# Turning u token-major with VectorE's 32 by 32 block transpose and a placing store, instead of TensorE's transpose through PSUM

## The chip, the cores and the metric

The kernel runs on one core of one Trainium2 chip. The metric is the device time of one execution in microseconds (us). Three executions of the kernel before took 592.72, 593.20 and 593.23 us: median 593.2.

## The reference

One decoder layer over 1024 tokens of width 1024, in float32. The normalised stream goes through one input projection into two head groups, a state-space layer (S5) and a latent attention (MLA); their outputs, 512 wide each, are concatenated, and then:

```python
mix = jnp.concatenate([ys, ym], axis=-1) @ w_out[i]
u = DEEPNORM_ALPHA * x + mix
ple = jax.nn.sigmoid(u @ w_pg[i]) * (p[i] @ w_pp[i])
x = layer_norm(u + ple, ln_g[i], ln_b[i])
```

So `u` is used twice: as an operand of the gate's matmul `u @ w_pg`, and as an addend beside the gate's result.

## The kernel before, in words

**Layout.** Up to the output projection everything is feature-major: 128 features on the partitions, tokens along the free axis. The gate's matmul makes token-major results (128 tokens on the partitions, 512 columns), and so does everything behind it. `u` is needed in both layouts: feature-major as the stationary operand of the gate's matmul, token-major as the addend. This case is about how the token-major copy is made.

**Precision.** Each float32 operand of a matmul is split into a high and a low part (`split`, line 511: a cast makes the high part, a subtraction the low one), and each product is three matmuls (`mm3`, line 518): high by high, high by low, low by high.

**Output projection (`out_proj`, line 1310).** There are eight blocks `m` of 128 features and two halves `hf` of 512 tokens. For each, 8 x 3 = 24 matmuls of 128x512 add up in one PSUM bank (`op`). VectorE then makes u in place in `xr` (`stt`, line 1319: alpha times the stream plus the bank), and `split` makes `uh` and `ul`, the operands of the gate. The weights `wor` and the stream `xr` are loaded two blocks ahead (`wo_load`), and the weights are split one block ahead (`wo_split`, to `woh` and `wol`).

**Token-major u (`u_tokens`, line 1322).** After both halves of a block, for each half: four TensorE transposes of 128x128 by an identity matrix into one PSUM bank (`ut`), one ScalarE copy from PSUM to the tile `ut` (128 tokens by 4 times 128 features), and one store of 256 KB to the DRAM tensor `d_ut`, whose rows are tokens. One row of this store is 128 features, 512 bytes.

**Gate (`gate`, line 1360).** For each of eight token blocks `t` and two column halves `c`, 8 x 3 = 24 matmuls (`g`), with the weights `wph` and `wpl` (loaded as `wpr`, four pieces for each column half, each of which serves two of the eight steps). ScalarE takes the sigmoid into `sgg`, VectorE multiplies it by the stored per-layer embedding (`ppr`) and adds the token-major u, which `u_load` (line 1352) loads back from `d_ut` as `utok` in 2 KB rows. `final` normalises the rows and stores the output. The first three token blocks run their column half 0 before their column half 1 (`GATE`, line 97).

**What sets the order.** The kernel doesn't issue its instructions directly. `Plan` (line 120) records all of them, with costs for each operation (`cost`), and `issue` (line 308) simulates the engines and writes down one order: at each step the earliest instruction that can start, with the written order as priority. Each engine then runs its own instructions strictly in that order. All DMAs go out on SyncE's queue (SP), also in order. Every DMA signals on one of eight completion semaphores in turn, and a DMA waits for the one issued eight before it.

**Buffers.** Tiles of 128x512 come from a pool of 12 (`Hf`), tiles of 128x1024 from a pool of 40 (`U`), the banks for `op` and `ut` from a pool of four (`PB`).

All instructions have line 441 in the profile, because the plan issues them there. So groups are told apart by the names of their tiles.

Of the kernel before, what the change touches and what calls it, by code (L numbers as in the profile page):

```python
# [34 lines left out]
P = 128  # L35
# [409 lines left out]
def trunk(ctx, tc, I, out):  # L445
    plan = Plan(tc)
    V, A, Gp, T, SY = plan.vector, plan.scalar, plan.gpsimd, plan.tensor, plan.sync
# [12 lines left out]
    def nm(s):  # L460
        cnt[0] += 1
        return f"{s}{cnt[0]}"
# [4 lines left out]
    def Hf(name, dt=F32, shape=(P, 512)):  # L467
        return plan.own(hp.tile(list(shape), dt, name=nm(name), tag="h"), "h", NHF)

    def C(name, shape, dt=F32):  # L470
        return cp.tile(list(shape), dt, name=nm(name), tag=nm(name))
# [7 lines left out]
    def PB(name, shape=(P, 512), dt=F32):  # L479
        return plan.own(psB.tile(list(shape), dt, name=nm(name), tag="B"), "B", 4)  # L480
# [27 lines left out]
    def cpy(e, o, a):  # L508
        plan.copy(e._name, o, a)
# [35 lines left out]
    def pexp(o, x, shape):  # L545
# [22 lines left out]
    ident = C("ident", (P, P))  # L568
    Gp.memset(ident, 1.0)
    Gp.affine_select(  # L570
        out=ident, in_=ident, pattern=[[-1, P]], compare_op=ALU.is_equal, fill=0.0, base=0, channel_multiplier=1
# [20 lines left out]
    d_ut = dr.tile([8, P, D], F32, name="d_ut")  # L592
# [702 lines left out]
    wo = {}  # L1295
# [24 lines left out]
        split(uT[m][0][:, s], uT[m][1][:, s], x[:, s])  # L1320

    def u_tokens(m, hf):
        x = wo[m][2]
        ps = PB("ut")
        for j in range(4):
            T.transpose(ps[:, j * P : j * P + P], x[:, hf * 512 + j * P : hf * 512 + j * P + P], ident)
        t = Hf("ut", shape=(P, 4, P))
        cpy(A, t, ps.rearrange("p (j c) -> p j c", j=4))
        SY.dma_start(out=d_ut[hf * 4 : hf * 4 + 4, :, m * P : m * P + P].rearrange("t p c -> p t c"), in_=t)


    wp = {}
# [189 lines left out]
    for i in range(n + 3):  # L1522
        if i < n:
            h, j = items[i]
            pr[i] = [scores(h, 2 * j + q) for q in range(2)]
        k = i - 1
        if 0 <= k < n:
            pts[k] = probs_t(*items[k], pr.pop(k))
        k = i - 2
        if 0 <= k < n:  # L1530
            os[k] = pv(*items[k], pts.pop(k))
        k = i - 3
# [3 lines left out]
    for m in range(NK):  # L1536
        if m + 2 < NK:
            wo_load(m + 2)
        if m + 1 < NK:
            wo_split(m + 1)  # L1540
        for hf in range(2):
            out_proj(m, hf)
        for hf in range(2):
            u_tokens(m, hf)
        if m == 6:
            for k in range(4):
                wp_load(0, k)
# [79 lines left out]
```

## Time and profile before

| what | value |
|---|---|
| the runs shown | 592.72 to 593.23 us, median 593.2 |
| the profiled execution itself | 592.97 us |
| its span, first to last instruction | 591.3 us |
| mean granted TensorE clock | 0.992 |
| busy: TensorE, VectorE, ScalarE, GpSimd | 567.1, 446.8, 281.6, 83.8 us |
| DMA traffic | 76.66 MB in 46233 packets |
| transposes `ut` on TensorE | 64, first at 411.9 us, last at 496.0 us |
| copies `ut` on ScalarE | 16, 588 ns each |
| stores `d_ut` | 16 of 256 KB, 2.4 us from issue to landing |

How to read it: the profiled execution takes 1.7 us more than its span, for what lies before its first and after its last instruction. Times in the views are counted from the span's start. A row of a timeline gives start, duration, engine and the operation as out<-in; in brackets, how long the engine had idled and for whom. PE is TensorE, PEld its weight loads, DVE VectorE, ACT ScalarE, POOL GpSimd, SP the queue of DMAs. Matmuls overlap, so the step from one to the next is less than the duration of one.

### The profile page before, as it was taken

To read this page: it belongs to the slowest core of one execution; us is meant where nothing else is said; L and a number is where in the kernel's file an instruction comes from. 1 tells how busy PE (TensorE), PEld (TensorE's weight loads), DVE (VectorE), ACT (ScalarE), POOL (GpSimd) and SP (SyncE) were. 2 spreads that over 40 slices of the span, in tenths; PEclk is the share of its full clock that TensorE was granted. 3 is DMA by queue.
4 is the path that set the end of the run, shared out by engine and by line. 5 is a ranking of instruction groups with operands and counts; after the bars stand their busy time and mean duration, and the time that the engine had idled before them with its cause. 6 is when DMAs were issued, how large, how long until landed. Compare 5 with 4: busy or idle time off the path is not lost.

```text
span 591.3 us, 8335 instructions
## 1 busy us (share of the span) xinstructions
PE 567.1 (96%) x3000; PEld 482.3 (82%) x3000; DVE 446.8 (76%) x952; ACT 281.6 (48%) x533; POOL 83.8 (14%) x100
## 2 busy tenths in 40 slices
PE   8989989999999999999999999899999999999994
PEld 6777868788898878878899998688888888888884
DVE  6999999989999986478989879876323226577666
ACT  5777136355383851367677786443222235133221
POOL 0000004201020234114522221010000010000000
PEclk9999989999999999999999999899999999999998
DMA  8897422532130512201013225326422438724301
GB/s 301 316 354 267 159 72 86 201 124 95 72 111 2 172 64 72 72 38 37 1 50 129 72 73 171 150 73 247 115 99 72 161 107 278 309 89 160 108 35 72
DMA packets 46233, 76.66 MB, mean 130 GB/s; under 512 B 4384, under 2 KB 27104, under 8 KB 46192
## 3 DMA queue, kind: packets, MB, share of 16 engines
q1 hardware_dynamic: 46192, 76.14, 37.3%
q8 instruction: 23, 0.38, 0.3%
q14 instruction: 18, 0.15, 0.1%
HBM read 50.47 MB, written 25.66 MB: 129 GB/s over the span
## 4 chain that ended last, share of the span: by engine, by line
PE 57%; DVE 4%; issue 1%; ACT 1%; DVEq 0%
PE op L441 15%; PE g L441 15%; PE s L441 6%; PE o L441 4%; PE z L441 4%; PE glu L441 3%; PE pt L441 2%; PE qn L441 2%; PE ut L441 1%; PE uv L441 1%; PE qrp L441 1%; DVE gsr L441 1%; PE y L441 1%; DVE p L441 1%; DVE hh L441 0%
## 5 line engine op out<-in xcount | busy, mean ns | idle before, releaser
L441 PE MATMUL z<-xh,wh 128*128 128x512 f32 x192 | 76.4, 398 | 1.2 <-DVE krh L441 1.2
L441 PE MATMUL z<-xh,wl 128*128 128x512 f32 x192 | 75.7, 396 | 1.1 <-DVE wl L441 1.1
L441 PE MATMUL z<-xl,wh 128*128 128x512 f32 x192 | 76.4, 398 | 0.0
L441 PE MATMUL g<-wph,uh 128*128 128x512 f32 (+1 forms) x136 | 51.4, 378 | 0.0
L441 PE MATMUL g<-wph,ul 128*128 128x512 f32 (+1 forms) x136 | 51.2, 377 | 0.0
L441 PE MATMUL g<-wpl,uh 128*128 128x512 f32 (+1 forms) x136 | 51.2, 377 | 0.0
L441 DVE SCALAR_TENSOR_TENSOR xr<-xr,op 128x512 f32<-128x512 f32 x16 | 11.0, 687 | 50.2 <-PE op L441 50.2
L441 PEld LDWEIGHTS z<-xh,wl 128*128 128x128 f32 x192 | 36.5, 190 | 8.6 <-DVE wl L441 1.7
L441 PEld LDWEIGHTS z<-xh,wh 128*128 128x128 f32 x192 | 36.5, 190 | 8.6 <-DVE krh L441 1.5
L441 PEld LDWEIGHTS z<-xl,wh 128*128 128x128 f32 x192 | 36.6, 190 | 6.9
L441 PEld LDWEIGHTS g<-wph,ul 128*128 128x128 f32 x136 | 25.6, 188 | 4.7
L441 PEld LDWEIGHTS g<-wpl,uh 128*128 128x128 f32 x136 | 25.6, 188 | 4.7
L441 PEld LDWEIGHTS g<-wph,uh 128*128 128x128 f32 x136 | 25.6, 188 | 4.6
L441 DVE CUSTOM_DVE_ANT_0 p<-s,mask 128x128 f32<-128x128 f32 (+7 forms) x32 | 23.8, 752 | 4.0 <-PE s L441 3.8
L441 ACT COPY ut<-ut 128x512 f32<-128x512 f32 x16 | 9.4, 588 | 35.3 <-PE ut L441 35.2
L441 PE MATMUL op<-ysh,woh 128*128 128x512 f32 x64 | 26.2, 409 | 0.0
L441 ACT ACTIVATE p<-p,mx 128x128 f32<-128x128 f32 (+7 forms) x32 | 24.8, 775 | 2.7 <-DVE mx L441 2.6
L441 DVE TENSOR_TENSOR ptl<-pt,pth 128x512 fp32r<-128x512 f32 (+3 forms) x48 | 25.3, 551 | 0.9 <-ACT pth L441 0.4
L441 ACT ACTIVATE sgg<-g 128x512 f32<-128x512 f32 (+1 forms) x17 | 9.6, 565 | 34.0 <-PE g L441 34.0
L441 PE MATMUL pt<-ident,p 128*128 128x128 f32 x144 | 21.5, 285 | 3.8 <-ACT sg L441 2.2
L441 PE MATMUL op<-ysh,wol 128*128 128x512 f32 x64 | 25.0, 391 | 0.0
L441 POOL TENSOR_TENSOR rstd<-ve,half 128x1 f32<-128x1 f32 (+1 forms) x10 | 7.1, 714 | 126.2 <-DVE ve L441 107.6
(370 smaller groups left out, 1673.1 us busy)
## 6 DMA issues: line engine op xcount, KB each, us to landing
wr<-in_w_fm SPq DMA_DIRECT2D x12, 512.0 KB, 5.6
x<-in_x SPq DMA_DIRECT2D x8, 512.0 KB, 8.7
d_pp<-ppo SPq DMA_DIRECT2D x8, 512.0 KB, 4.8
d_xln<-xt SPq DMA_DIRECT2D x16, 256.0 KB, 6.1
wor<-in_w_out SPq DMA_DIRECT2D x8, 512.0 KB, 5.8
xr<-d_xln SPq DMA_DIRECT2D x8, 512.0 KB, 5.2
d_ut<-ut SPq DMA_DIRECT2D x16, 256.0 KB, 2.4
utok<-d_ut SPq DMA_DIRECT2D x16, 256.0 KB, 4.2
```

Source lines behind the costliest of these rows:

```text
L441: getattr(self.real[ran[i]], method)(*ops[i]["args"], **kw)
```

## The change

`u_tokens` no longer uses TensorE, PSUM and ScalarE. VectorE transposes the 128x512 half of `xr` in one instruction, within blocks of 32 by 32: element (32a + k, 32b + i) of the source goes to (32a + i, 32b + k). Partition 32a + i of the tile then holds, for each of the 16 token groups b, the 32 features of feature group a for token 32b + i. Four stores, one for each feature group a, place these runs of 32 features (128 bytes) into the rows of `d_ut`: each store takes 32 partitions and moves 512 runs, 64 KB. `d_ut` holds the same as before, and the loads `utok` are the same. The plan is not edited; it makes its order anew from the changed list of instructions.

```diff
     def u_tokens(m, hf):
-        x = wo[m][2]
-        ps = PB("ut")
-        for j in range(4):
-            T.transpose(ps[:, j * P : j * P + P], x[:, hf * 512 + j * P : hf * 512 + j * P + P], ident)
-        t = Hf("ut", shape=(P, 4, P))
-        cpy(A, t, ps.rearrange("p (j c) -> p j c", j=4))
-        SY.dma_start(out=d_ut[hf * 4 : hf * 4 + 4, :, m * P : m * P + P].rearrange("t p c -> p t c"), in_=t)
+        t = Hf("ut")
+        V.transpose(t, wo[m][2][:, hf * 512 : hf * 512 + 512])
+        for a in range(4):
+            o = d_ut[hf * 4 : hf * 4 + 4, :, m * P + 32 * a : m * P + 32 * a + 32]
+            SY.dma_start(
+                out=o.rearrange("t (b i) k -> i (t b) k", i=32),
+                in_=t[32 * a : 32 * a + 32].rearrange("i (b k) -> i b k", k=32),
+            )
```

In the order of the changed kernel the transposes appear on VectorE as `STREAM_TRANSPOSE ut<-xr`, the stores on SP as four `d_ut<-ut` of 32x16x32.

## The prediction

> **What bounds the kernel now.** First the page: its first part gives the engines' shares, its fourth the chain that ended last.
>
> ```profile
> span 591.3 us, 8335 instructions
> PE 567.1 (96%) x3000; PEld 482.3 (82%) x3000; DVE 446.8 (76%) x952; ACT 281.6 (48%) x533; POOL 83.8 (14%) x100
> PE op L441 15%; PE g L441 15%; PE s L441 6%; PE o L441 4%; PE z L441 4%; PE glu L441 3%; PE pt L441 2%; PE qn L441 2%; PE ut L441 1%; PE uv L441 1%; PE qrp L441 1%; DVE gsr L441 1%; PE y L441 1%; DVE p L441 1%; DVE hh L441 0%
> ```
>
> TensorE sets the time, and the transposes that the change removes (`ut`) stand on the chain themselves, with 1% of it. The change touches one stage, the output projection, so I read that stage alone: the table of stretches (the four busy columns are PE, weight loads, DVE, ACT, then POOL; after them granted clock, DMA share, GB/s), and the chain in order of time.
>
> ```profile
> 401.00:496.00 95.00, 95.00 (x451) 78.74 (x451) 33.69 (x45) 26.32 (x41) 3.50 (x2) 1.00 0.41 138
> 401.10 10.91 PE op L441 x48
> 413.58 10.23 PE op L441 x45
> ...
> 484.46 10.24 PE op L441 x45
> 496.28 86.71 PE g L441 x405
> ```
>
> In these 95 us TensorE is busy throughout at a granted clock of 1.00; VectorE works 33.7 us, ScalarE 26.3, the DMA engines have 41% of their time filled. The chain is `op` with small holes, then 86.7 us of `g` without one. The holes are `ut`. So time taken from TensorE here is time taken from the kernel, as long as nothing else becomes late.
>
> **What is removed from TensorE.** The price is not the duration of a transpose, because matmuls overlap; it is what the next matmul is pushed back. TensorE's timeline:
>
> ```profile
> 400.94 0.40 PE L441 MATMUL op<-ysh,woh 128*128 128x512 f32 x1
> ...
> 411.62 0.40 PE L441 MATMUL op<-ymh,wol 128*128 128x512 f32 x1
> 411.85 0.60 PE L441 MATMUL ut<-ident,xr 128*128 128x128 f32 x4
> 412.20 0.48 PE L441 MATMUL op<-ysh,woh 128*128 128x512 f32 x1
> ...
> 494.54 0.60 PE L441 MATMUL ut<-ident,xr 128*128 128x128 f32 x4
> 494.90 0.48 PE L441 MATMUL g<-wph,uh 128*128 128x512 f32 x1
> ```
>
> From 400.94 to 411.62 lie 47 steps without a transpose: 10.68 / 47 = 0.2272 us a matmul. The first group of `ut` of block 0 starts at 411.85, that of block 7 at 494.54: (494.54 - 411.85) / 7 = 11.81 us a block. A block has 48 matmuls, 10.91 us, so its two groups of transposes cost 0.906 us. Eight blocks: **7.25 us**. (64 transposes at their mean duration would be 17 us; that is no saving, since most of it overlaps.) The order of TensorE where the stage ends and the gate begins (`op` is the last projection group, `g` the first gate group, `ut` the transposes), before:
>
> ```order
> L441 MATMUL op_1186<-ymh_1036,wol_1170 128x512
> L441 MATMUL ut_1187<-ident_75,xr_1158 128x128 x4
> L441 MATMUL g_1203<-wph_1191,uh_1102 128x512
> L441 MATMUL g_1203<-wpl_1192,uh_1102 128x512
> L441 MATMUL g_1203<-wph_1191,ul_1103 128x512
> L441 MATMUL ut_1189<-ident_75,xr_1158 128x128 x4
> L441 MATMUL g_1203<-wph_1191,uh_1114 128x512
> ```
>
> and with the change:
>
> ```order
> L441 MATMUL op_1172<-ymh_1036,wol_1158 128x512
> L441 MATMUL g_1187<-wph_1175,uh_1102 128x512
> L441 MATMUL g_1187<-wpl_1176,uh_1102 128x512
> L441 MATMUL g_1187<-wph_1175,ul_1103 128x512
> L441 MATMUL g_1187<-wph_1175,uh_1112 128x512
> ```
>
> Nothing but `ut` has gone; all other matmuls keep their order. The gate would then start at 400.94 + 384 x 0.2272 = 488.2 instead of 494.9 (the last group of `ut` lies behind three gate matmuls).
>
> ScalarE loses 16 copies out of PSUM. Worth nothing by itself: ScalarE waits for TensorE before them.
>
> ```profile
> L441 ACT COPY ut<-ut 128x512 f32<-128x512 f32 x16 | 9.4, 588 | 35.3 <-PE ut L441 35.2
> ```
>
> **What VectorE gets.** 16 transposes of 128x512 f32. The trace has none; the bounds are a one-input cast, the fastest row of this size, and four times a 128-element scan, the slowest per element:
>
> ```profile
> L441 DVE CAST uh<-xr 128x512 fp32r<-128x512 f32 x1 | 0.4, 426 | 0.0
> L441 DVE SCALAR_TENSOR_TENSOR xr<-xr,op 128x512 f32<-128x512 f32 x15 | 10.3, 687 | 49.2 <-PE op L441 49.2
> L441 DVE TENSOR_TENSOR ul<-xr,uh 128x512 fp32r<-128x512 f32 x15 | 10.4, 692 | 11.0 <-ACT uh L441 11.0
> L441 DVE TENSOR_TENSOR wol<-wor,woh 128x1024 fp32r<-128x1024 f32 x6 | 7.8, 1309 | 0.0
> L441 DVE TENSOR_TENSOR_SCAN rt<-mg,rt 128x128 f32<-128x128 f32 x32 | 12.1, 442 | 0.0
> ```
>
> So 0.43 to 1.77 us; I take 0.69, the f32 rate of most rows. A block asks of VectorE 2 x 0.687 + 2 x 0.692 + 1.309 = 4.1 us, with two transposes 5.4, at most 7.6, of 10.9 us: hidden. In each half the transpose is issued ahead of `ul`, so `ul` and what follows slip by 0.69. In most blocks no one soon needs `ul`. The one tight place is the start of the gate, whose first group needs the low parts `wpl` of the gate weights. VectorE's order there, before:
>
> ```order
> L441 SCALAR_TENSOR_TENSOR xr_1158<-xr_1158,op_1183 128x512
> L441 TENSOR_TENSOR ul_1185<-xr_1158,uh_1184 128x512
> L441 TENSOR_TENSOR wpl_1194<-wpr_1180,wph_1193 128x1024
> L441 TENSOR_TENSOR wpl_1196<-wpr_1181,wph_1195 128x1024
> L441 SCALAR_TENSOR_TENSOR xr_1158<-xr_1158,op_1186 128x512
> L441 TENSOR_TENSOR wpl_1198<-wpr_1182,wph_1197 128x1024
> ```
>
> and with the change:
>
> ```order
> L441 SCALAR_TENSOR_TENSOR xr_1148<-xr_1148,op_1169 128x512
> L441 STREAM_TRANSPOSE ut_1173<-xr_1148 128x512
> L441 TENSOR_TENSOR ul_1171<-xr_1148,uh_1170 128x512
> L441 TENSOR_TENSOR wpl_1178<-wpr_1166,wph_1177 128x1024
> L441 TENSOR_TENSOR wpl_1180<-wpr_1167,wph_1179 128x1024
> L441 SCALAR_TENSOR_TENSOR xr_1148<-xr_1148,op_1172 128x512
> L441 TENSOR_TENSOR wpl_1182<-wpr_1168,wph_1181 128x1024
> L441 TENSOR_TENSOR ul_1171<-xr_1148,uh_1170 128x512
> ```
>
> Block 7's second transpose moved behind all this; its first stands ahead of two `wpl`. In the trace:
>
> ```profile
> 489.30 0.69 DVE L441 SCALAR_TENSOR_TENSOR xr<-xr,op 128x512 f32<-128x512 f32 x1 [4.10 <-PE op L441]
> 490.73 0.69 DVE L441 TENSOR_TENSOR ul<-xr,uh 128x512 fp32r<-128x512 f32 x1 [0.74 <-ACT uh L441]
> 491.34 2.35 DVE L441 TENSOR_TENSOR wpl<-wpr,wph 128x1024 fp32r<-128x1024 f32 x2
> ```
>
> VectorE idles 0.74 us there for ScalarE's `uh`, room for a 0.69 us transpose. The two `wpl` end 4.4 us after `xr` began, and `xr` begins one group, 24 x 0.2272 = 5.45 us, ahead of the gate: they end some 1.0 us before it. Each `wpl` serves six matmuls of a gate group; these two are first read by the 8th and the 14th, 1.6 and 3.0 us into it. So a transpose of 1.77 us, 1.0 more than fits, still costs nothing; TensorE would wait only beyond some 4.5 us. Term: 0.
>
> **What the stores become.** 16 stores of 256 KB in 512-byte rows become 64 of 64 KB in 128-byte runs, four per half block, all on SP's queue. Issue, from two loads issued back to back, is 0.455 us each; 64 of them 29 us of an 80 us stage. SP's order at the stage's end (`wpr` are gate weights, `utok` the loads that read the stored tokens back), before:
>
> ```order
> L441 DMA wpr_1182<-in_w_pg 128x1024
> L441 DMA d_ut<-ut_1176 128x4x128
> L441 DMA d_ut<-ut_1178 128x4x128
> L441 DMA ppr_1199<-d_pp 128x1024
> L441 DMA wpr_1200<-in_w_pg 128x1024
> ```
>
> and with the change:
>
> ```order
> L441 DMA wpr_1168<-in_w_pg 128x1024
> L441 DMA d_ut<-ut_1163 32x16x32 x4
> L441 DMA d_ut<-ut_1164 32x16x32 x4
> L441 DMA d_ut<-ut_1173 32x16x32 x4
> L441 DMA ppr_1183<-d_pp 128x1024
> L441 DMA wpr_1184<-in_w_pg 128x1024
> ```
>
> The weights for the gate's second column half are now queued behind block 7's first stores as well, and the last two of them also behind the `utok` loads that wait until those stores have landed. A store takes 2.4 us from issue to landing now. The price of a 128-byte packet written to DRAM is in no row. The nearest are the 512-byte stores of now (436 to 440 us, two `d_ut`) and a load with 128-byte rows (24 to 25 us, `fr`), and for the rate of large loads the stretch from 497.4:
>
> ```profile
> 450.86 0.91 SPq L441 DMA_DIRECT2D utok<-d_ut  x2
> ...
> d_ut<-ut SPq DMA_DIRECT2D x16, 256.0 KB, 2.4
> ...
> q1 hardware_dynamic: 1056, 0.52, 43.6%
> ...
> fr<-in_inv_freq SPq DMA_DIRECT2D x1, 16.0 KB, 2.5
> q1 hardware_dynamic: 153, 0.02, 11.9%
> ...
> 497.40:503.00 5.60, 5.60 (x27) 4.62 (x26) 3.68 (x4) 3.05 (x4) 0.00 (x0) 1.00 1.04 364
> ```
>
> 0.436 x 4 us x 16 engines / 1056 = 26.4 ns a packet of 512 bytes; 0.119 x 1 us x 16 / 153 = 12.4 ns a packet of 128 (16 KB in 128 rows, the rest signals). Each store has 512 data packets, 32 an engine, and one that signals: 33. At 12.4 ns all 64 take 26 us of each engine, at 26.4 ns 56 us, against 14 us now. I take about 20 ns, between the two rows, 42 us: it fits beside the loads, and no load is late.
>
> The page "DMA: Bandwidth & Descriptors" of the Trainium skill (Specifications) speaks against the change here: under 512 bytes a transfer is not at line rate, because the DMA engine reads, modifies and writes. If that doubled the 26.4 ns of the larger packet, the first rival below would come true; if it doubled 12.4 ns, the sum would stay. No run here shows it yet.
>
> **Sum.** 592.97 us (the profiled execution, of which 591.3 are its span) - 7.25 + 0 + 0 = 585.7. The median of the runs shown is 0.2 us above the profiled one, so I forecast **585.9 us**.
>
> **Rivals.**
>
> *The small stores fill the DMA engines, and the gate waits for weights: slower.* Stores could start at 407.8 (400.94, one group of 5.45, `xr` and a transpose of 0.69 each). Ahead of the last two gate weights stand 60 stores and, with these two, 18 times 512 KB of loads (two `wor`, two `xr`, eight `wpr`, three `ppr`, six `utok` of half the size), at 364 GB/s 1.44 us each, 26 us. With 2 us of latency, and 2.3 for the split of the weights (a cast and a subtraction, rows below), they are ready at 438.1 + 60 x 0.033 x p, p in ns. They are wanted three groups and six steps into the gate, 488.2 + 16.4 + 4.1 = 508.7. Nothing is late below p = 36; the whole gain is gone at 39; at 52.8 (twice the measured 512-byte packet) the wait is 34 us, so 620 us.
>
> ```profile
> L441 ACT CAST wph<-wpr 128x1024 fp32r<-128x1024 f32 x4 | 4.0, 1052 | 0.0
> L441 DVE TENSOR_TENSOR wpl<-wpr,wph 128x1024 fp32r<-128x1024 f32 x2 | 2.4, 1218 | 0.0
> ```
>
> For it: a write is not the load that gave 12.4 ns, and all runs of one store lie at multiples of 4 KB. Against: it takes three times the price of a 128-byte load. Chance 0.12.
>
> *Part of the gain is lost at the gate's start,* to late `wpl` or late gate weights at p between 36 and 39: up to 6 us lost, 587.4 to 592. Against: the margins above. Chance 0.08.
>
> *The change does nothing for the time:* another engine ends the stage where TensorE did. VectorE would need 3.4 us a transpose (10.9 - 4.1, halved); the slowest row says 1.77. 593 us, chance 0.05.
>
> **How the numbers follow.** The forecast, 584.3 to 587.4, has 0.75; its low end lets more close up than the 7.25 us read from the block starts, its high end lets 1.5 us go at the gate. A measurement of this kernel tells 0.2%, 1.2 us, from no change: faster 0.75 + 0.08, same 0.05, slower 0.12. The range 584.3 to 590.0 leaves out the first and third rival and half of the second, near 0.2.
>
> **What would show it.** Right: `ut` gone from TensorE, `op` as one run of 384 matmuls at 0.227 us, `g` from about 488, a transpose near 0.69 us, VectorE still waiting for `op`, packets of 128 bytes at 12 to 27 ns. Wrong: holes in `g` that end with a `wpr` landing or `wph`, a DMA share near 1 from 410 on, `d_ut` landings far above the present 2.4 us, or TensorE waiting for `wpl`.

## The result, and the profile after

The changed kernel takes **585.19 us** (median of four executions, 584.48 to 586.96); the kernel before, run beside it, 592.96. The ratio is 0.987, interval 0.985 to 0.988: some 7.8 us faster. The forecast was 585.9, in a range of 584.3 to 590.0.

The execution profiled took 585.17 us. Its page: the first line, the two lines on TensorE and on DMA traffic that differ most from before, and the shares of the chain.

```profile
span 583.5 us, 8264 instructions
PE 559.1 (96%) x2936; PEld 475.9 (82%) x2936; DVE 457.5 (78%) x968; ACT 272.8 (47%) x517; POOL 83.6 (14%) x100
DMA packets 71577, 76.67 MB, mean 131 GB/s; under 512 B 37920, under 2 KB 52448, under 8 KB 71536
PE g L441 15%; PE op L441 15%; PE s L441 6%; PE z L441 4%; PE o L441 4%; PE glu L441 3%; PE pt L441 2%; PE qn L441 2%; PE uv L441 1%; PE qrp L441 1%; DVE gsr L441 1%; PE y L441 1%; DVE p L441 1%; DVE hh L441 0%; PE qrt L441 0%
```

TensorE has 64 instructions fewer, VectorE 16 more, ScalarE 16 fewer. The same bytes go in 25,000 packets more. `ut` has left the chain. In order of time the chain through both stages is now two rows:

```profile
401.06 87.07 PE op L441 x384
488.13 87.36 PE g L441 x408
```

Before, the same matmuls stood in pieces with the transposes between them, and the last long piece of `g` began at 496.28. The table of stretches (PE, weight loads, DVE, ACT, POOL, clock, DMA share, GB/s) over the projection:

```profile
401.00:488.00 87.00, 87.00 (x386) 72.03 (x385) 41.93 (x57) 18.40 (x26) 3.51 (x2) 1.00 0.55 134
```

TensorE is busy throughout, as it was, in a stretch 8 us shorter. VectorE has 8.2 us more and ScalarE 7.9 less. The DMA engines are at 0.55 instead of 0.41. To find where the time went, I take the first `op` and the fourth gate matmul (in both kernels nothing of `ut` comes after it). TensorE's timeline:

```profile
400.90 0.40 PE L441 MATMUL op<-ysh,woh 128*128 128x512 f32 x1
...
487.96 0.39 PE L441 MATMUL g<-wph,uh 128*128 128x512 f32 x1
488.64 0.39 PE L441 MATMUL g<-wph,uh 128*128 128x512 f32 x1
```

and the same gate matmul before (the first `op` of before, at 400.94, is shown in the prediction):

```profile
496.04 0.47 PE L441 MATMUL g<-wph,uh 128*128 128x512 f32 x1
```

From 400.90 to 488.64 are 87.74 us; before, from 400.94 to 496.04, 95.10. The stretch is 7.36 us shorter, 0.460 for each of the 16 groups. From there to the end of the gate's chain it is 86.85 against 86.95, and the tail behind it 8.01 against 8.31. Together 7.36 + 0.10 + 0.30 + 0.04 (the earlier start) = 7.80, the difference of the two spans.

### The profile page after: what moved, and what is told of

Its sections match the earlier page's. It is cut to its first block, busy times and chain, and to the rows that moved or that the text cites. A ratio compares the mean times of both kernels' runs of the same rounds, so it can differ in the third digit from the quotient of the medians.

```text
span 583.5 us, 8264 instructions
## 1 busy us (share of the span) xinstructions
PE 559.1 (96%) x2936; PEld 475.9 (82%) x2936; DVE 457.5 (78%) x968; ACT 272.8 (47%) x517; POOL 83.6 (14%) x100
## 4 chain that ended last, share of the span: by engine, by line
PE 56%; DVE 5%; issue 1%; ACT 1%; DVEq 0%
PE g L441 15%; PE op L441 15%; PE s L441 6%; PE z L441 4%; PE o L441 4%; PE glu L441 3%; PE pt L441 2%; PE qn L441 2%; PE uv L441 1%; PE qrp L441 1%; DVE gsr L441 1%; PE y L441 1%; DVE p L441 1%; DVE hh L441 0%; PE qrt L441 0%
## 5 line engine op out<-in xcount | busy, mean ns | idle before, releaser
L441 DVE SCALAR_TENSOR_TENSOR xr<-xr,op 128x512 f32<-128x512 f32 x16 | 11.0, 686 | 39.1 <-PE op L441 39.1
L441 ACT CAST uh<-xr 128x512 fp32r<-128x512 f32 x16 | 9.9, 621 | 64.8 <-DVE xr L441 51.5
L441 PE MATMUL op<-ysh,woh 128*128 128x512 f32 x64 | 24.9, 389 | 0.0
L441 PE MATMUL op<-ysl,woh 128*128 128x512 f32 x64 | 24.9, 389 | 0.0
L441 PE MATMUL op<-ymh,woh 128*128 128x512 f32 x64 | 24.9, 389 | 0.0
L441 PE MATMUL op<-yml,woh 128*128 128x512 f32 x64 | 24.9, 389 | 0.0
```

What stands on the lines that cost most here:

```text
L441: getattr(self.real[ran[i]], method)(*ops[i]["args"], **kw)
```

## The experiments

**The theory:** the whole gain is TensorE's time, 0.45 us for each group of four transposes that TensorE no longer does. VectorE's transpose and the 64 small stores lie beside other work and cost nothing. **Rivals:** the gain is larger, and VectorE's transpose or the stores give part of it back; or it comes from ScalarE's copies; or the stage is close to being bound by VectorE, by packets or by the issue of stores.

**How they are compared.** The spans differ by up to 3.8 us before the projection starts, in a part whose instructions stand in the same order in all these kernels: there the granted clock varies, 0.97 to 1.00 between 300 and 400 us. So beside the medians stands the time from the first `op` to the end of the span ("rest"), from the profiled executions, and, as a part of it, the time from the first `op` to the fourth gate matmul ("stage"). The ratios are to the kernel before as it was run beside each kernel (medians 592.41 to 594.01).

| run | first `op` | span | rest | stage | median | ratio to before |
|---|---|---|---|---|---|---|
| before | 400.9 | 591.3 | 190.4 | 95.10 | 592.96 | 1 |
| after | 400.9 | 583.5 | 182.6 | 87.74 | 585.19 | 0.985 to 0.988 |
| e4_te_back | 400.7 | 590.8 | 190.1 | 95.12 | 592.99 | 0.997 to 1.001 |
| e3_half | 402.2 | 588.7 | 186.5 | 91.58 | 590.40 | 0.990 to 0.995 |
| e2_no_turn | 401.3 | 584.2 | 182.9 | 87.75 | 585.81 | 0.983 to 0.988 |
| e1_rows | 404.4 | 587.2 | 182.8 | 87.74 | 587.34 | 0.984 to 0.991 |
| e5_turn_x4 | 401.4 | 584.0 | 182.6 | 87.74 | 585.44 | 0.985 to 0.989 |
| e5_turn_x8 | 400.8 | 585.5 | 184.7 | 87.74 | 587.43 | 0.989 to 0.992 |
| e6_store_x2 | 400.6 | 583.2 | 182.6 | 87.74 | 585.77 | 0.986 to 0.990 |
| e6_store_x4 | 401.9 | 641.0 | 239.1 | 110.30 | 642.49 | 1.081 to 1.085 |
| e7_packets_a | 401.4 | 584.3 | 182.9 | 87.74 | 586.52 | 0.988 to 0.993 |
| e8_packets_b | 402.4 | 627.8 | 225.4 | 100.19 | 629.26 | 1.058 to 1.063 |

All edits are to the changed kernel's `u_tokens`.

### Is it TensorE's time?

**e4_te_back:** the transposes on TensorE come back, into a bank that nobody reads; no copy, and the new transposes and stores stay.

```diff
+        x = wo[m][2]
+        ps = PB("ut")
+        for j in range(4):
+            T.transpose(ps[:, j * P : j * P + P], x[:, hf * 512 + j * P : hf * 512 + j * P + P], ident)
         t = Hf("ut")
         V.transpose(t, wo[m][2][:, hf * 512 : hf * 512 + 512])
```

> The changed kernel, with TensorE's 64 transposes put back beside VectorE's; nobody reads their PSUM banks, and ScalarE's 16 copies and the 512-byte stores stay away. Theory (the gain is TensorE's own time, 16 groups of 0.45 us): 592.4 to 593.2 us, all of the gain gone, no difference to the kernel before. Rival (ScalarE's copies, the PSUM banks held by them, or the new order of the queues bring part of it): clearly under 591 us.

Measured: 592.99 us, ratio 0.997 to 1.001, rest 190.1, stage 95.12 against 95.10 before. The whole gain is gone, though the copies are not back. The chain at the first two blocks and at the gate:

```profile
400.90 10.92 PE op L441 x48
411.82 0.44 PE ut L441 x4
412.25 0.70 PE op L441 x3
412.95 0.44 PE ut L441 x4
...
496.10 86.71 PE g L441 x405
```

Each group of `ut` stands on the chain with 0.44 us, and each leaves the next matmul some 0.02 us later. TensorE waits for nothing else in the stage, so the PSUM banks that `ut` takes up again cost nothing either. So ScalarE's copies were worth nothing, and the new transposes and stores cost nothing.

**e3_half:** the first half of each block in the old way, the second in the new.

```diff
+        if hf == 0:
+            x = wo[m][2]
+            ps = PB("ut")
...
+        else:
+            t = Hf("ut")
+            V.transpose(t, wo[m][2][:, hf * 512 : hf * 512 + 512])
...
```

> Half 0 of every block turned as before (TensorE, PSUM, ScalarE, one store), half 1 as in the changed kernel. Theory: the cost is a fixed one for each group of four transposes, so half of the 7.8 us: 588.9 to 589.5 us. Rival (the gain hangs on one place, such as the start of the gate): near 585 or near 593 us, not between.

Measured: rest 186.5, the middle of 190.4 and 182.6; stage 91.58, 3.84 above the changed kernel's. The median, 590.40, is above what I expected, by about as much as the projection of the profiled execution starts late (1.3 us). The chain:

```profile
402.40 10.91 PE op L441 x48
413.31 0.44 PE ut L441 x4
...
493.28 87.42 PE g L441 x408
```

One group for each block is left, again 0.44 us. The gain is in proportion to the groups removed.

### What do VectorE's transpose and the small stores cost?

**e2_no_turn:** no transpose anywhere; the half of `xr` is stored as it is, in rows of 512 bytes, so `d_ut` no longer holds u by tokens.

```diff
-        t = Hf("ut")
-        V.transpose(t, wo[m][2][:, hf * 512 : hf * 512 + 512])
...
+        x = wo[m][2][:, hf * 512 : hf * 512 + 512]
+        SY.dma_start(out=d_ut[hf * 4 : hf * 4 + 4, :, m * P : m * P + P].rearrange("t p c -> p t c"), in_=x.rearrange("p (j c) -> p j c", j=4))
```

> Leaves the turning out: the feature-major half goes to the scratch tensor as it is, in one store of 512-byte rows, so that neither VectorE nor TensorE nor ScalarE does anything for it. Theory (VectorE's transposes and the small runs are hidden): 584.8 to 585.8 us, the same as the changed kernel. Rival (either of them costs something on the path): faster than the changed kernel, by 1 us or more.

**e1_rows:** the transpose stays, but one store of 256 KB in rows of 512 bytes takes the place of the four; the blocks are not placed.

```diff
-        for a in range(4):
...
+        SY.dma_start(out=d_ut[hf * 4 : hf * 4 + 4, :, m * P : m * P + P].rearrange("t p c -> p t c"), in_=t.rearrange("p (j c) -> p j c", j=4))
```

> VectorE's transposes stay, but each half is stored by one DMA of 256 KB in 512-byte rows, without placing the blocks (the placing is left out). Theory (64 stores of 128-byte runs take some 10 us more of each DMA engine, none of it waited for): 584.8 to 585.8 us, the same as the changed kernel. Rival (the four stores for each half delay something by their issue or their landing): faster than the changed kernel by 1 us or more.

Measured: rest 182.9 and 182.8, against 182.6 with everything; the stage is the same in all three (87.74 to 87.75), and the 0.3 lies behind VectorE's last instruction. The median of e1_rows, 587.34, is above what I expected. Its profiled execution, the slowest of four (588.96), starts the projection at 404.4; of the other three (585.29 to 588.56) no trace was kept. The stretches of e2_no_turn, then those of e1_rows:

```profile
401.00:488.00 87.00, 87.00 (x387) 72.09 (x386) 32.93 (x44) 18.21 (x25) 3.48 (x2) 1.00 0.45 143
```

```profile
404.50:491.50 87.00, 87.00 (x386) 72.01 (x385) 41.99 (x57) 18.44 (x26) 3.50 (x2) 1.00 0.44 140
```

VectorE's column falls by 9 us without the transposes, and the DMA share by 0.1 without the small stores. TensorE's column doesn't move. Neither of the two new costs is on the path.

### How far off are they?

**e5_turn_x4 and e5_turn_x8:** the transpose is done 4 or 8 times (below with 8).

```diff
-        V.transpose(t, wo[m][2][:, hf * 512 : hf * 512 + 512])
+        for _ in range(8):
+            V.transpose(t, wo[m][2][:, hf * 512 : hf * 512 + 512])
```

> Each of VectorE's transposes done four times over (2.85 us a half at 0.712 us each); the result is the same. Theory (VectorE has 5.45 us a half and some 2.0 us of other work; at the start of the gate 3.8 us may slip): nothing is waited for, 584.8 to 586.2 us. Rival (the margin at the gate is less, or the transposes hold up other engines): slower than the changed kernel by 2 us or more, with waits for wpl or ul in g.

> Each of VectorE's transposes done eight times over (5.7 us a half; with xr 6.4 us, against the 5.45 us that TensorE needs for a half). The plan moves ul and wol to GpSimd. Theory: VectorE becomes the bound of the stage, 16 x 0.9 = 15 us more or beyond, 599 to 615 us. Rival (TensorE is buffered well enough by the four PSUM banks for this to stay hidden): under 590 us.

Measured: 4 times cost nothing (rest 182.6), 8 times 2.1 us (184.7). For 8 my theory fell: it took 6.4 us for a half, a sum of durations, and let the excess over 5.45 count in full. The stretch, GpSimd's group in it, and rows of VectorE's timeline:

```profile
401.00:488.00 87.00, 87.00 (x385) 72.01 (x385) 85.55 (x137) 17.50 (x26) 28.09 (x19) 1.00 0.49 128
```

```profile
L441 POOL TENSOR_TENSOR ul<-xr,uh 128x512 fp32r<-128x512 f32 x14 | 18.2, 1298 | 56.7 <-ACT uh L441 46.7 <-issue 9.8 <-PE op L441 0.2
```

```profile
407.33 0.68 DVE L441 SCALAR_TENSOR_TENSOR xr<-xr,op 128x512 f32<-128x512 f32 x1
...
469.18 4.85 DVE L441 STREAM_TRANSPOSE ut<-xr 128x512 f32<-128x512 f32 x8
...
489.97 0.66 DVE L441 SCALAR_TENSOR_TENSOR xr<-xr,op 128x512 f32<-128x512 f32 x1
```

VectorE is full (85.6 of 87 us), and yet TensorE is busy for all 87. Two things let it. The plan has moved the subtractions `ul` to GpSimd. And VectorE's instructions overlap too: eight transposes in a row take 4.84 to 5.46 us here, not eight times a duration. From the first `xr` to the last, VectorE takes (489.97 - 407.33) / 15 = 5.51 us a half, where TensorE gives it 24 x 0.2272 = 5.45. So it hardly falls behind: each `xr` begins 0.5 to 2.4 us after the last matmul of its half, the last one 1.9 us after it. The wait comes only at the gate, for a `wpl` that GpSimd makes behind the last `ul` (TensorE's timeline; in brackets the wait and for whom):

```profile
487.67 0.39 PE L441 MATMUL op<-ymh,wol 128*128 128x512 f32 x1
...
495.06 0.50 PE L441 MATMUL g<-wpl,uh 128*128 128x512 f32 x1 [1.11 <-POOL wpl L441]
```

With that wait the gate takes 1.5 us more than in the changed kernel; the other 0.6 of the 2.1 lies behind VectorE's last instruction, and I know no cause for it.

**e6_store_x2 and e6_store_x4:** each store is made again, once or three times, to DRAM tensors that nobody reads.

```diff
-            SY.dma_start(
-                out=o.rearrange("t (b i) k -> i (t b) k", i=32),
...
+            for d in (o, *(e[hf * 4 : hf * 4 + 4, :, m * P + 32 * a : m * P + 32 * a + 32] for e in d_ux)):
+                SY.dma_start(
+                    out=d.rearrange("t (b i) k -> i (t b) k", i=32),
...
```

> Each of the 64 stores issued twice, the second to a spare tensor that nobody reads: 128 stores. In the changed kernel's trace a 128-byte packet takes 11.6 ns of an engine, so this is as if one took 23 ns, and 128 issues of 0.49 us are 63 us of an 80 us stage. Theory (nothing is late below 36 ns a packet, 0.7 us of issue for each of 64): 584.8 to 586.5 us. Rival (the margin is smaller than was worked out, by the queue's order or the eight stores in flight): slower than the changed kernel by 2 us or more.

> Each of the 64 stores issued four times, three of them to spare tensors: 256 stores, as if a packet took 46 ns, and 256 issues of 0.49 us are 125 us against a stage of 87 us. Theory: the last gate weights are late, by 438 + 60 x 0.033 x 46 - 509 = 20 us if the DMA engines bind, by 408 + 240 x 0.49 + 18 x 0.45 + 7 - 509 = 32 us if the issue on SP binds; 605 to 618 us, with holes in g that end with a wpr. Rival (the loads find their way past the stores, or the plan moves them ahead): under 592 us.

Measured: 128 stores cost nothing (rest 182.6); 256 cost 56 us (239.1). Stretches of e6_store_x2:

```profile
401.00:488.00 87.00, 87.00 (x386) 72.01 (x385) 41.67 (x58) 18.25 (x26) 3.48 (x2) 1.00 0.78 171
```

and of e6_store_x4, with its SP queue (start, duration of the issues) and its chain:

```profile
409.00:505.00 96.00, 80.17 (x354) 66.06 (x352) 33.17 (x48) 11.78 (x18) 0.00 (x0) 0.93 0.72 131
```

```profile
409.71 1.59 SPq L441 DMA_DIRECT2D d_ux<-ut  x3
411.35 0.49 SPq L441 DMA_DIRECT2D d_ut<-ut  x1
411.88 1.58 SPq L441 DMA_DIRECT2D d_ux<-ut  x3
...
505.14 0.46 SPq L441 DMA_DIRECT2D wpr<-in_w_pg  x1
```

```profile
559.43 5.03 DMA wpr<-in_w_pg
```

With twice the stores of e6_store_x2 the DMA share isn't higher, 0.72 against 0.78: the engines aren't the limit. SP is. It issues four stores in 2.17 us (409.71 to 411.88), 0.54 each. The first gate weights go out at 505.1, where they went out at 459.0 in the changed kernel; TensorE's longest wait, 21.6 us up to 510.8, is for them. The last four stand behind 240 stores, 130 us at this pitch, and go out from 559.4 on. The waits of this kernel that show it (us in total, times, longest):

```profile
ACT wph L441 <- DMA wpr<-in_w_pg: 69.5, 8, 24.6
...
PE g L441 <- ACT wph L441: 43.2, 4, 21.6
```

The kind of loss was foreseen, its size was under: 43 of the 56 us are these waits, and 3.2 are one for `sgg`. The others fall together with a granted clock that drops once TensorE idles, 0.93 in the stretch above against 1.00; what it costs I did not separate.

**e7_packets_a and e8_packets_b:** one more store for each half, to a tensor that nobody reads, in pieces of 32 bytes: 4096 pieces in the first (below), 8192 in the second. That adds many packets and only 16 issues.

```diff
+        SY.dma_start(out=d_ux[2 * m + hf][:, :, 0:8], in_=t[:, 0 : 256].rearrange("p (r k) -> p r k", k=8))
```

> The changed kernel with one more store for each half block: 4096 pieces of 32 bytes of the same tile to a spare tensor that nobody reads. Only 16 more issues on SP, but 256 more packets for each DMA engine and half: with the 11.6 ns of the changed kernel's stores 48 us more of each engine, as if every packet of the 64 stores took 34 ns. Theory (the engines have room up to 36 ns): 584.8 to 588 us. Rival (stores four times over were slow because the DMA engines were full, and that happens earlier than worked out): slower than the changed kernel by 5 us or more.

> The same with 8192 pieces of 32 bytes for each half block: 95 us more of each DMA engine, as if a packet took 57 ns, still only 16 more issues. Theory (the DMA engines are the second limit, beyond 36 ns, by the sum of the prediction's first rival): 438 + 60 x 0.033 x 57 - 509 = 42 us late, 615 to 635 us, with holes in g that end with gate weights. Rival (only the issue on SP can be a limit): under 592 us.

Measured: 4096 pieces cost 0.3 us from the projection on (rest 182.9), 8192 cost 43 us (225.4). Stretches of e7_packets_a:

```profile
407.00:488.00 81.00, 81.00 (x359) 67.11 (x358) 36.28 (x51) 15.98 (x22) 2.42 (x1) 1.00 0.90 134
```

and of e8_packets_b, with its waits:

```profile
407.00:488.00 81.00, 81.00 (x359) 67.10 (x358) 34.47 (x49) 12.44 (x18) 0.00 (x0) 1.00 0.94 104
488.00:530.00 42.00, 21.73 (x64) 15.25 (x63) 6.01 (x7) 5.12 (x6) 2.34 (x1) 0.67 0.96 114
```

```profile
PE g L441 <- ACT wph L441: 26.0, 4, 9.5
PE g L441 <- DVE wpl L441: 4.0, 5, 1.6
PE g L441 <- POOL wpl L441: 1.6, 1, 1.6
```

With the DMA engines 90% busy, the stage is as long as in the changed kernel. Once the work in front of the weights no longer ends in time, it still doesn't show in the projection (TensorE is busy 81 of 81 us) but behind it, where the gate waits for weights: 32 of the 43 us. The rest again goes with the granted clock, 0.67 there.

The 0.3 us of e7_packets_a are the beginning of this. The last `wpl` and the matmul that first reads it, in the changed kernel, then in e7_packets_a:

```profile
502.49 1.22 DVE L441 TENSOR_TENSOR wpl<-wpr,wph 128x1024 fp32r<-128x1024 f32 x1
508.59 0.39 PE L441 MATMUL g<-wpl,uh 128*128 128x512 f32 x1
```

```profile
508.02 1.22 DVE L441 TENSOR_TENSOR wpl<-wpr,wph 128x1024 fp32r<-128x1024 f32 x1
509.29 0.50 PE L441 MATMUL g<-wpl,uh 128*128 128x512 f32 x1
```

In the changed kernel the weights are ready 4.9 us ahead of their reader (before the change 9.8); in e6_store_x2 1.8 us; in e7_packets_a they end at 509.24, where the matmul before, at 508.93, would have let their reader start at 509.16, and the gate loses 0.3 us. This is the place that the prediction's first rival names, three groups and six steps into the gate.

Which resource is the limit, these two runs do not separate. In e8_packets_b the DMA engines are full (0.94), but SP is full too: from 410.5 to 536.8 its queue is free for under 8 us in all, since the issue behind a store of 8192 pieces takes 3 to 6 us, as for this `wpr` (0.43 in the changed kernel, at 459.0):

```profile
489.10 4.81 SPq L441 DMA_DIRECT2D wpr<-in_w_pg  x1
```

## Why the prediction was right, step by step

**TensorE's term: right.** 7.25 us were worked out, 7.36 came. e4_te_back takes all of it back, e3_half one half. That also settles the term for ScalarE's copies, 0: they aren't back in e4_te_back.

**VectorE's transpose: right in size and in cover.** It takes 0.712 us where 0.69 was taken (groups of the changed kernel, 401 to 488):

```profile
L441 DVE STREAM_TRANSPOSE ut<-xr 128x512 f32<-128x512 f32 x15 | 10.7, 712 | 0.7
L441 DVE SCALAR_TENSOR_TENSOR xr<-xr,op 128x512 f32<-128x512 f32 x15 | 10.3, 687 | 39.1 <-PE op L441 39.1
```

VectorE still waits 39.1 us for `op`, 49.2 before. e2_no_turn shows that taking the transposes out gains nothing.

**The margin at the gate: wrong in size, without a cost.** The step said that VectorE's 0.74 us of idling for `uh` makes room for the transpose, so that the two `wpl` end 1.0 us before the gate starts. They end at 486.16 + 2.35 = 488.51, 0.55 after its first matmul. ScalarE's timeline at this place before, then after, then VectorE's after:

```profile
490.07 0.62 ACT L441 CAST uh<-xr 128x512 fp32r<-128x512 f32 x1 [3.09 <-DVE xr L441]
490.66 2.01 ACT L441 CAST wph<-wpr 128x1024 fp32r<-128x1024 f32 x2
```

```profile
483.40 1.05 ACT L441 CAST wph<-wpr 128x1024 fp32r<-128x1024 f32 x1 [2.75 <-PE op L441]
484.37 0.61 ACT L441 CAST uh<-xr 128x512 fp32r<-128x512 f32 x1
```

```profile
482.72 0.69 DVE L441 SCALAR_TENSOR_TENSOR xr<-xr,op 128x512 f32<-128x512 f32 x1 [2.30 <-PE op L441]
483.45 0.71 DVE L441 STREAM_TRANSPOSE ut<-xr 128x512 f32<-128x512 f32 x1
485.01 1.23 DVE L441 TENSOR_TENSOR ul<-xr,uh 128x512 fp32r<-128x512 f32 x1 [0.85 <-ACT uh L441]
486.16 2.35 DVE L441 TENSOR_TENSOR wpl<-wpr,wph 128x1024 fp32r<-128x1024 f32 x2
```

Before, ScalarE made `uh` as soon as `xr` was there, and the `wph` behind it. In the new order one `wph` stands ahead of `uh`. So `uh` comes later too, VectorE idles 0.85 us for it behind its transpose as well, and the room that I had filled was not there: I read the order of VectorE alone, and the release of `ul` sits on ScalarE. The second of the two `wpl` is read by the 14th matmul, at 487.96 + 13 x 0.2272 = 490.9, 2.4 us after it was ready. This second margin, which the prediction named as well, is why the term stayed 0.

**The packets: inside the bounds, at their cheap end.** In a stretch in which only `d_ut` stores move (419.5 to 431.5; packets, MB, share of 16 engines):

```profile
q1 hardware_dynamic: 5193, 0.65, 31.3%
```

0.313 x 12 us x 16 / 5193 = **11.6 ns** a packet. I took 20, between 12.4 (a 128-byte load) and 26.4 (a 512-byte store); the row of the same packet size was the better guide, not the row of the same direction. A store lands 1.9 us after its issue, 2.4 before. The page "DMA: Bandwidth & Descriptors" of the Trainium skill (Specifications) says that transfers under 512 bytes are read, modified and written, below line rate. The measurement bears out half of it: per byte these packets are 1.8 times dearer (11.6 / 128 against 26.4 / 512 ns), but a packet isn't dearer than a 128-byte load, so no reading and writing back shows in its time.

**The first rival: such a loss exists, its condition is not met.** It was to decide from 36 ns a packet. With one more store for each half, by its sum as if a packet took 34 ns, the last weights are 0.3 us late (e7_packets_a); the sum put the limit at 36. With twice the pieces the gate waits (e8_packets_b). For packets as cheap as they came the sum is no measure of the margin: at 11.6 ns it has the weights ready at 438.1 + 60 x 0.033 x 11.6 = 461, as if all the work lay ready at 407.8, but the last four go out only from 486.8 on, and the margin is 4.9 us. What it left out is the issue, where I took 0.455 us: at 0.54, 64 stores are 35 us of SP's 80, and it is SP, not the engines, that more stores like these fill first (e6_store_x4).

**The third rival: threshold too low.** VectorE was to bind at 3.4 us a transpose. Eight of them, 4.84 to 5.46 us, left the stage as it was and cost 1.5 us at the gate. The sum counted `ul` and `wol` as VectorE's in any case, and the plan moves `ul` and part of `wol` to GpSimd.

**The sum.** For the profiled execution 585.7 was worked out and 585.17 came. Of the 0.5 us between, 0.11 is TensorE's term, 0.1 the gate, and 0.3 the tail behind the gate. That 0.3 was in no term, and its cause stays open. It lies behind VectorE's last instruction (587.9 to 591.3 before, 580.4 to 583.5 after), where only the last stores of the output are left. It doesn't come from the transposes on TensorE, for e4_te_back has the short tail too (582.81 to 590.8, 7.99); e1_rows and e2_no_turn, with one store for each half, have the long one (8.3), and e5_turn_x8 a longer one still (8.6).

## What to carry to other kernels

Where one engine is busy throughout a stage, price an instruction taken from it by the step that it takes out of the engine's timeline, not by its duration: 0.45 us for four transposes that last 1.1. The same goes for the engine that gets the work: eight of VectorE's transposes took 4.84 to 5.46 us, not 8 x 0.712 = 5.7. Before work goes to an engine with idle time, follow what releases its next instruction on the other engines as well, since a new order can move that release. For many small stores count issues as well as packets, and look for the loss behind the stage, where the loads queued after the stores are first wanted.

## What the runs showed of the hardware

- A 128-byte packet stored to DRAM took 11.6 ns on its DMA engine, no more than a loaded one (12.4).
- SP issued 64 KB stores of 512 runs one every 0.54 us in a long row. In e6_store_x4 that, and not the DMA engines (0.72), was the limit.
- The issue that followed a store of 8192 pieces of 32 bytes on SP's queue took 3 to 6 us (e8_packets_b); a load of gate weights took 4.81 there and 0.43 in the changed kernel. What holds it, the full engines or the making of the pieces, is not shown.
- Where TensorE had to wait for weights its granted clock fell as well, to 0.67 in a stretch of e8_packets_b, and the loss (43 us) was larger than the waits (32).
- VectorE's transpose within 32 by 32 blocks of 128x512 f32 takes 0.712 us, about as long as other f32 operations of that size (0.687); eight in a row took 4.84 to 5.46 us, 0.61 to 0.68 each.
- With VectorE 98% busy (85.55 of 87 us) in a stage (e5_turn_x8), TensorE didn't wait in it: VectorE began each half at most 2.4 us after TensorE had ended it.
